# Inverting 16 by 16 blocks instead of 8 by 8 on VectorE, with other costs in the list scheduler

## The chip, the cores and the metric

The kernel runs on one core of one Trainium2 chip. The metric is device time in microseconds (us); a kernel is run several times and the median counts. A profile is one further execution, recorded by the hardware profiler.

The engines are TensorE (PE, with its weight loads as PEld), VectorE (DVE), ScalarE (ACT), GpSimd (POOL) and SyncE (SP), which here issues nearly all DMAs. In the kernel's code they are `T`, `V`, `S`, `G` and `Y`.

## What is computed

One decoder layer for 256 prompt tokens (one sequence) and 64 sample tokens (8 sequences of 8), 320 tokens in all. The model width is 2048. A single projection `h @ w_in` feeds two branches, whose outputs are projected, gated, added and projected once more. Branch A is a delta rule over 16 heads of 64:

```python
def step(s, inp):
    r_t, w_t, k_t, v_t, kk_t, a_t = inp
    sa = jnp.einsum('nhvk,nhk->nhv', s, kk_t)
    s = (s * w_t[:, :, None, :]
         - sa[..., None] * (kk_t * a_t)[:, :, None, :]
         + v_t[..., None] * k_t[:, :, None, :])
    return s, jnp.einsum('nhvk,nhk->nhv', s, r_t)
...
merged = (jax.nn.sigmoid(p[..., OFF_GA:OFF_GB]) * (y_a @ proj_a)
          + jax.nn.sigmoid(p[..., OFF_GB:]) * (y_b @ proj_b))
y = x + merged @ w_out
```

Branch B is a gated linear recurrence over 8 heads of 128. All inputs and outputs are fp32.

## The kernel before

**Weights.** Every large product is made of three: weights and activations are each split into a high and a low part of the type fp32r (`whi`, `wlo`, `hhi`, `hlo`), and high x high, high x low and low x high are added in PSUM. A block of weights is 1024 x 128: SyncE loads `raw` (512 KB), ScalarE rounds it to `whi`, VectorE subtracts to get `wlo`, and TensorE runs 24 matmuls of 128 x 128 by 320 tokens into `mps`. There are three buffers of each.

**Stages.** After a start (norm and transposes of x) comes the *recorded stage*, which goes to about 690 us. It runs over p = 0 to 7; one p is two heads of branch A and one of branch B and is called a head below. For each p eight column tiles of `w_in` (two blocks each) are streamed, then come `rwkv(p, ...)` and `hgrn(p, ...)`. Seven tiles of gate columns (`NFILL` + `NLATE`) follow as filler. Then the last stage streams the other gates, `proj_a`, `proj_b` and `w_out`; it needs `ya` and `yb`, the branches' outputs, of all heads.

**The order of the recorded stage.** All its instructions are first recorded by `Recorder`, with the regions that each reads and writes. `Recorder.order` then plays them through in time: each has a `cost` (how long its engine is taken) and a `lat` (how long until another may use its result), PE products that are not streamed have a `margin`, and for each engine the ready instruction with the highest `worth` (for most the `rank`, the length of the longest chain behind it) is taken next. Streamed matmuls keep their order and fill TensorE where nothing else is ready. The resulting order of each engine is fixed in the program, SyncE's DMAs included. All these instructions are issued at L1465, so the profile gives that line for the stage, and groups are told apart by tile names. Tags shared by several tiles show as the tag (`uB`, `uE`, `uK`, `pp`, `big`).

**The inverse.** Within a chunk of 64 tokens (and within a sample sequence of 8) the delta rule needs the inverse of I + N, N strictly triangular. The steps in `rwkv`:

- `g2` holds the masked products of keys, `nd` their part for the inverse, `M` its transpose.
- GpSimd masks the diagonal blocks of 8 (`lows`, a tile of `pp`), VectorE sums them into `dn` (128 partitions x 6 x 8). Two DMAs through a scratch tensor in DRAM turn that into `nb`: 96 partitions, one whole 8 by 8 block each.
- VectorE makes `y8` = `id8` - `nb`, and inverts: four instructions join 1 by 1 blocks to 2 by 2, then two products and two reduces join 4 by 4 blocks to 8 by 8 (`t64`, `p16`).
- Two DMAs bring the blocks back as `ye`; GpSimd spreads them into `yd` (prompt) and `ys` (samples), ScalarE copies `yd` into `yz`.
- A loop over `sz` in 8, 16, 32 joins blocks of `sz` to blocks of twice that on TensorE: two transposes of `yd`, a copy to `xt` (tag `uB`), the product `M` x `yz` (`pP`), the masked product `pp` on VectorE, the product `xt` x `pp` (`pD`), two subtractions from `yz` on VectorE and, except the last time, two copies to `yd` on ScalarE.

Then the chunks follow one another (`rhs`, `uv`, the states `st`), and the result is normalised and gated into `ya`.

Of the kernel before, what the change touches and what calls it, by code (L numbers as in the profile page):

```python
# [67 lines left out]


class Recorder:  # L70
    APART, MARGIN, WAIT, OVER = 10, 250, 6000, 130
    LAT = {"PE": 215, "V": 45, "S": 45, "G": 80, "Y": 0}

    def __init__(self, engines, is_big):
        self.real, self.ops, self.spans, self.is_big = engines, [], {}, is_big
# [10 lines left out]
    def add(self, eng, name, fn, args, kw):  # L86
        o = Op()
        o.eng, o.fn, o.args, o.kw, o.n = eng, fn, args, kw, len(self.ops)
        aps = [x for x in (*args, *kw.values()) if hasattr(x, "start_partition")]
        out = aps[0]  # L90
        free = 1
        for d in out.shape[1:]:
            free *= d
        o.uses = []
        for j, x in enumerate(aps):
            t_ = x.tensor
            if "DRam" in type(t_).__name__:
# [12 lines left out]

        two = sum("PSUM" not in str(x.space) for x in aps[1:] if tuple(x.shape[1:]) != (1,)) > 1
        o.hold = two and eng in "VG"
        o.port = two and eng == "V" or eng == "G" and "dma" not in name
        if eng == "PE":
            lhs, rhs = aps[1], aps[2]
            o.cols = 1
            for d in lhs.shape[1:]:
                o.cols *= d
            n = 1
            for d in rhs.shape[1:]:  # L120
                n *= d
# [12 lines left out]
        elif eng == "V":  # L134
            two = name in ("tensor_scalar", "tensor_copy") and all(not u[5] for u in o.uses)
            o.cost = (free / 2 if two else free) / 0.96 + (150 if two else 157)
            if two:
                o.hold = o.port = True
            if any(tuple(x.shape[1:]) == (1,) and free > 1 for x in aps[1:]):
                o.cost += 55  # L140
            if name == "tensor_tensor_scan":
                o.cost = 2 * free / 0.96 + 157
        elif eng == "S":
            o.cost = (150 if name == "copy" else 200) + free / 1.2
            if name == "copy" and not o.uses[1][5]:
                o.cost += 40
            if any(tuple(x.shape[1:]) == (1,) and free > 1 for x in aps[1:]):
                o.cost += 60
        elif eng == "G":
            o.cost = 950 if "dma" in name else 95 + free * 0.88 if name == "memset" else 200 + free * 1.66  # L150
            if "dma" in name:
                o.lat = 4500
        else:
            o.cost, o.lat = 380, 2600 if any(u[0].startswith("scr") for u in o.uses) else 5500
        self.ops.append(o)
        return o

    def link(self):
# [42 lines left out]
        for o in self.ops:  # L201
            o.npred = len(preds[o.n])
            for q, data in preds[o.n].values():
                q.succ.append((o, data))
        for o in reversed(self.ops):
            o.rank = o.cost + max((q.rank + (o.lat if data else 0) for q, data in o.succ), default=0)
        for members in groups.values():
# [4 lines left out]
    def order(self):  # L212
# [12 lines left out]
        at = {}  # L225
# [4 lines left out]
        def choose(e):  # L230
# [12 lines left out]
            if e == "PE":  # L243
# [13 lines left out]
                if o.stream:  # L257
                    o = min((o for o in pool if o.stream), key=lambda o: o.n)
                return max(t_, o.ready), o
            can = [o for o in q if (at_[o] if e in port else o.ready) <= t_ + 30]  # L260

            def worth(o):
                if o.block is None:
                    return (3 if e == "Y" else 1), o.rank
                slack = (at[o.block] - gone) * 147 + max(0, free["PE"] - t_)
                return (2 if slack < 4500 else 0), -o.n
            return t_, max(can, key=worth)

        while left:
            t_, o = min((choose(e) for e in ready if ready[e]), key=lambda x: (x[0], x[1].eng == "V"))  # L270
# [27 lines left out]
def hybrid_step(ctx, tc, x_prompt, x_sample, state_rwkv, state_hgrn, state_shift, norm_g, w_in,  # L298
# [80 lines left out]
    with tc.tile_pool(name="start", bufs=1) as st, \  # L379
# [60 lines left out]
            G.affine_select(out=ap, in_=ap, pattern=pattern, compare_op=ALU.is_ge, fill=fill,  # L440
                            base=base, channel_multiplier=cm)

        id8 = ctile([128, 64], "id8")
        G.memset(id8, 0.0)
        G.memset(id8[:, 0:64:9], 1.0)
        id32 = ctile([128, 32], "id32")
        G.tensor_add(id32, id64[:, 0:32], id64[:, 32:64])


        low_ = HS[0]  # L450
        lvs = st.tile([128, 3, 32], F32, name="lvs")
        lvz = ctile([128, 3, 2, 32], "lvz")
        seqm = ctile([128, NSEQ], "seqm")
        mk_lv = {}
        V.memset(lvs[low_], 1.0)
        G.memset(seqm[low_], 1.0)
        for n, sz in enumerate((8, 16, 32)):
            mk_lv[sz] = lvz[:, n]
            lv = lvs[low_, n].rearrange("p (b s) -> p b s", s=sz)
            nb = 32 // sz  # L460
# [6 lines left out]
        V.memset(lvz[low_, :, 1], 0.0)  # L467
        V.memset(lvz[HS[1], :, 0], 0.0)
        G.tensor_copy(seqm[HS[1]], seqm[low_])

# [314 lines left out]
    def rwkv(p, r, k, vp, za):  # L785
# [132 lines left out]
        for h in range(2):  # L918
            for c_ in range(2):
                S.copy(M[HS[c_], :, h], ps[HS[h], :256].rearrange("p (a c s) -> p a c s", c=2, s=64)[:, :, c_])  # L920


        lows = at("lows", (128, 4, 8, 8), tag="pp")
        each = lambda n: seqm[:, None, :, None].to_broadcast([128, n, 8, 8])
        G.tensor_mul(lows, nd.rearrange("p a h (b j) -> p (a h) b j", j=8), each(4))
        dn = at("dn", (128, 6, 8))
        V.tensor_reduce(dn[:, 0:4], lows.rearrange("p c b j -> p c j b"), axis=mybir.AxisListType.X, op=ALU.add)
        V.tensor_reduce(dn[0:64, 4:6], g2[0:64, 4, 0].rearrange("p h (b j) -> p h j b", j=8),
                        axis=mybir.AxisListType.X, op=ALU.add)
        there = lambda t_: t_.rearrange("(c p) j -> p c j", c=6)  # L930
        whole = lambda t_: t_.rearrange("(q i) j -> q (i j)", i=8)
        Y.dma_start(there(scratch[0]), dn)
        nb = at("nb", (96, 64), tag="pp")
        Y.dma_start(nb, whole(scratch[0]))
        y8 = at("y8", (96, 64))
        V.tensor_sub(y8, id8[:96], nb)

        t8 = nb
        four = lambda o_, *d: bass.AP(y8.tensor, y8.offset + o_, [y8.ap[0], *d])
        t4 = t8[:, 0:4].rearrange("p (a i) -> p a i", i=2)  # L940
        V.tensor_mul(t4, four(2, [36, 2], [8, 2]), four(19, [36, 2], [0, 2]))
        V.tensor_add(four(3, [36, 2], [8, 2]), four(3, [36, 2], [8, 2]), t4)
        V.tensor_mul(t4, four(10, [36, 2], [1, 2]), four(1, [36, 2], [0, 2]))
        V.tensor_add(four(2, [36, 2], [1, 2]), four(2, [36, 2], [1, 2]), t4)
        t64 = t8.rearrange("p (i j k) -> p i j k", j=4, k=4)
        p16 = at("p16", (96, 4, 4))
        V.tensor_mul(t64, four(4, [8, 4], [0, 4], [1, 4]), four(36, [0, 4], [1, 4], [8, 4]))
        V.tensor_reduce(p16, t64, axis=mybir.AxisListType.X, op=ALU.add)
        V.tensor_mul(t64, four(0, [8, 4], [0, 4], [1, 4]),
                     p16.rearrange("p k j -> p j k")[:, None].to_broadcast([96, 4, 4, 4]))  # L950
        V.tensor_reduce(four(4, [8, 4], [1, 4]), t64, axis=mybir.AxisListType.X, op=ALU.add)
        Y.dma_start(whole(scratch[1]), y8)
        ye = at("ye", (128, 6, 8))
        Y.dma_start(ye, there(scratch[1]))

        ys = at("ys", (128, 2, 64))
        wide = lambda t_: t_.rearrange("p h (b j) -> p h b j", j=8)
        spread = lambda x, n: ye[x, 4 * (n == 2):4 * (n == 2) + n, None, :].to_broadcast([x.stop - x.start, n, 8, 8])
        G.tensor_mul(yd.rearrange("p a h (b j) -> p (a h) b j", j=8), spread(slice(0, 128), 4), each(4))
# [14 lines left out]

        for sz in (8, 16, 32):
            xt = at("xt", (128, 4, 64), tag="uB")
            px = aps("pX")
            for cp in range(2):  # L980
# [703 lines left out]
```

## Time and profile before

| | |
|---|---|
| median of 3 runs | 1105.28 us (1103.35 to 1106.14) |
| profiled execution | 1104.54 us |
| its span, from the first to the last instruction | 1102.8 us |
| mean granted TensorE clock | 0.996 |
| TensorE busy | 1081.3 us, 98% of the span |
| VectorE busy | 750.6 us, 68% |
| ScalarE busy | 680.1 us, 62% |
| GpSimd busy | 154.6 us, 14% |

Durations of the trace are those of the profiled execution. A row that groups instructions has their line, engine, operation, tiles (out<-in), shape and count, then the busy time in us and the mean duration in ns, then the idle time of the engine just before them and what ended most of it. A row of the order of time begins with the start and the duration in us. A wait row has the total in us, the number of waits and the longest.

### The profile page before, as it was taken

How to read it: one execution, taken by the hardware profiler on the slowest of the kernel's cores; microseconds unless marked ns; L12 is line 12 of the kernel's file. 1: busy time of each engine (PE TensorE's matmuls, PEld its weight loads, DVE VectorE, ACT ScalarE, POOL GpSimd, SP SyncE). 2: the span in 40 equal slices, each digit the busy share in tenths (PEclk: the TensorE clock that was granted, in tenths of full speed). 3: DMA queues.
4: the chain of work that ended last, by engine and by line, in shares of the span. 5: the costliest groups of instructions: out<-in, count | busy, mean ns of one | idle time of the engine just before them, and what ended most of it. 6: DMA issues, size and time to landing. Idle time of an engine off the chain costs nothing.

```text
span 1102.8 us, 23134 instructions
## 1 busy us (share of the span) xinstructions
PE 1081.3 (98%) x9020; PEld 1043.5 (95%) x9020; DVE 750.6 (68%) x1639; ACT 680.1 (62%) x1530; POOL 154.6 (14%) x328
## 2 busy tenths in 40 slices
PE   7999999999999999999999999999999999999996
PEld 6999999999998999999999999999999999998886
DVE  8878787888787788788887976644444444437532
ACT  8767776766865867857857867544444444435412
POOL 6421222311211211211311210000000000000000
PEclk9999999999999999999999999999999999999999
DMA  6743644654553554555445454555555555586502
GB/s 200 205 127 100 180 129 123 161 145 114 162 136 101 156 144 117 153 138 140 117 138 144 123 144 130 149 152 160 152 146 146 149 154 153 153 282 223 200 21 96
DMA packets 298386, 161.62 MB, mean 147 GB/s; under 512 B 37341, under 2 KB 288480, under 8 KB 297700
## 3 DMA queue, kind: packets, MB, share of 16 engines
q1 hardware_dynamic: 297908, 158.83, 50.1%
q8 instruction: 71, 1.16, 0.4%
q10 hardware_dynamic: 368, 1.31, 0.3%
q14 instruction: 39, 0.32, 0.1%
HBM read 149.41 MB, written 10.70 MB: 145 GB/s over the span
## 4 chain that ended last, share of the span: by engine, by line
PE 95%; ACT 2%; DMA 1%; DVE 1%; issue 0%; POOL 0%; DVEq 0%; SPq 0%; ACTq 0%
PE mps L1465 45%; PE a L1465 9%; PE mps L362 5%; PE mps L364 5%; PE mps L363 5%; PE b L1465 3%; PE po L1555 3%; PE po L1556 3%; PE po L1557 3%; PE ppa L363 2%; PE ppa L364 2%; PE ppa L362 2%; PE ppb L362 2%; PE ppb L363 2%; PE ppb L364 2%; PE y L1465 1%
## 5 line engine op out<-in xcount | busy, mean ns | idle before, releaser
L1465 PE MATMUL mps<-hhi,wlo 128*128 128x320 f32 x1136 | 358.9, 316 | 0.0
L1465 PE MATMUL mps<-hhi,whi 128*128 128x320 f32 x1136 | 357.0, 314 | 0.5 <-ACT pad L1465 0.5
L1465 PE MATMUL mps<-hlo,whi 128*128 128x320 f32 x1136 | 357.3, 314 | 0.0
L1465 PEld LDWEIGHTS mps<-hhi,wlo 128*128 128x128 f32 x1136 | 213.7, 188 | 2.3 <-issue 1.5
L1465 PEld LDWEIGHTS mps<-hhi,whi 128*128 128x128 f32 x1136 | 213.8, 188 | 2.0 <-issue 0.8
L1465 PEld LDWEIGHTS mps<-hlo,whi 128*128 128x128 f32 x1136 | 213.7, 188 | 1.5 <-issue 0.8
L1465 DVE TENSOR_TENSOR wlo<-raw,whi 128x1024 fp32r<-128x1024 f32 x140 | 173.6, 1240 | 21.0 <-ACT whi L1465 19.7
L1465 ACT CAST whi<-raw 128x1024 fp32r<-128x1024 f32 x140 | 146.4, 1045 | 63.2 <-PE mps L1465 56.7
L352 ACT CAST whi<-raw 128x1024 fp32r<-128x1024 f32 x82 | 86.0, 1049 | 147.8 <-PE mps L363 94.3
L353 DVE TENSOR_TENSOR wlo<-raw,whi 128x1024 fp32r<-128x1024 f32 x82 | 100.5, 1225 | 110.1 <-ACT whi L352 110.1
L362 PE MATMUL mps<-hhi,whi 128*128 128x320 f32 x400 | 123.9, 310 | 1.0 <-ACT whi L352 1.0
L364 PE MATMUL mps<-hhi,wlo 128*128 128x320 f32 x400 | 123.7, 309 | 0.2 <-DVE wlo L353 0.2
L363 PE MATMUL mps<-hlo,whi 128*128 128x320 f32 x400 | 123.8, 309 | 0.0
L362 PEld LDWEIGHTS mps<-hhi,whi 128*128 128x128 f32 x400 | 75.1, 188 | 1.3 <-ACT whi L352 1.3
L364 PEld LDWEIGHTS mps<-hhi,wlo 128*128 128x128 f32 x400 | 75.1, 188 | 0.4 <-DVE wlo L353 0.4
L363 PEld LDWEIGHTS mps<-hlo,whi 128*128 128x128 f32 x400 | 75.2, 188 | 0.0
L1544 DVE TENSOR_TENSOR wlo<-raw,whi 128x1024 fp32r<-128x1024 f32 x32 | 38.4, 1222 | 36.0 <-ACT whi L1543 35.8
L1543 ACT CAST whi<-raw 128x1024 fp32r<-128x1024 f32 x32 | 33.1, 1052 | 47.7 <-PE po L1560 21.1
L1555 PE MATMUL po<-whi,mhi 128*128 128x512 f32 x128 | 50.0, 391 | 0.0
L1556 PE MATMUL po<-whi,mlo 128*128 128x512 f32 x128 | 50.0, 391 | 0.0
L1557 PE MATMUL po<-wlo,mhi 128*128 128x512 f32 x128 | 50.0, 391 | 0.0
L362 PE MATMUL ppa<-yah,whi 128*128 128x320 f32 x128 | 40.1, 314 | 0.1
(444 smaller groups left out, 2100.2 us busy)
## 6 DMA issues: line engine op xcount, KB each, us to landing
raw<-in_w_in_dram SPq DMA_DIRECT2D x194, 512.0 KB
raw<-in_w_out_dram SPq DMA_DIRECT2D x32, 512.0 KB
raw<-in_proj_a_dram SPq DMA_DIRECT2D x16, 512.0 KB
raw<-in_proj_b_dram SPq DMA_DIRECT2D x16, 512.0 KB
s<-in_state_hgrn_dram SPq DMA_DIRECT2D x8, 512.0 KB
out_dram<-s SPq DMA_DIRECT2D x8, 512.0 KB
s<-in_state_rwkv_dram SPq DMA_DIRECT2D x8, 256.0 KB
out_dram<-s SPq DMA_DIRECT2D x8, 256.0 KB
```

The source lines that it names most:

```text
L352: S.copy(hi[:, ks], raw[:, ks])
L353: sub.tensor_sub(lo[:, ks], raw[:, ks], hi[:, ks].bitcast(F32))
L362: T.matmul(dst, hi[:, q, :], xhi[:, k, :], start=(k == 0), stop=False)
L363: T.matmul(dst, hi[:, q, :], xlo[:, k, :], start=False, stop=False)
L364: T.matmul(dst, lo[:, q, :], xhi[:, k, :], start=False, stop=(k == nk - 1))
L1465: o.fn(*o.args, **o.kw)
L1543: S.copy(hi, raw)
L1544: V.tensor_sub(lo, raw, hi.bitcast(F32))
L1555: T.matmul(pt, h, hi, start=first, stop=False)
L1556: T.matmul(pt, l, hi, start=False, stop=False)
L1557: T.matmul(pt, h, lo, start=False, stop=end)
```

## The change

Two things are changed together.

The blocks that VectorE inverts are 16 by 16. `own16` replaces the mask of 8; the tiles become `dn` 128 x 6 x 16, `nb` and `y16` 48 x 256, `ye` 128 x 6 x 16, and the scratch tensors 768 x 16. A sample sequence's 8 by 8 blocks are inverted in pairs, as 16 by 16 blocks with zeros beside them. The negation of `nb` is a tensor_scalar, and GpSimd writes the ones of the diagonal. The 2 by 2 step covers twice the columns; the product-and-reduce step runs for n = 4 on two blocks and for n = 8 on one. The loop on TensorE runs over 16 and 32 only.

In `Recorder`, 85 ns (VectorE), 100 ns (ScalarE) and 65 ns (GpSimd) are taken off the cost of each instruction and added to its latency, which is also counted on every edge to another engine; the other latencies and the overlap of the port that VectorE and GpSimd share (`OVER`) get new values. A tensor_reduce costs as many elements as it reads. In the choice of the next instruction, one that becomes ready within 150 ns (`AHEAD`) may be preferred to one that is ready now; a shorter one goes first only where it ends at most 60 ns (`SLIP`) past the preferred one's start.

```diff
 class Recorder:
-    APART, MARGIN, WAIT, OVER = 10, 250, 6000, 130
-    LAT = {"PE": 215, "V": 45, "S": 45, "G": 80, "Y": 0}
+    APART, MARGIN, WAIT, OVER = 10, 250, 6000, 45
+    AHEAD, SLIP = 150, 60
+    LAT = {"PE": 215, "V": 40, "S": 40, "G": 65, "Y": 0}
+    DRAIN = {"V": 85, "S": 100, "G": 65}
...
+        if eng in self.DRAIN and not o.dma:
+            if name == "tensor_reduce":
+                n = 1
+                for d in aps[1].shape[1:]:
+                    n *= d
+                o.cost += (n - free) / 0.96
+            o.cost -= self.DRAIN[eng]
+            o.lat += self.DRAIN[eng]
...
-                q.succ.append((o, data))
+                q.succ.append((o, data or q.eng in self.DRAIN and q.eng != o.eng))
...
-            can = [o for o in q if (at_[o] if e in port else o.ready) <= t_ + 30]
+            if e not in port:
+                at_ = {o: max(now, o.ready) for o in q}
...
-            return t_, max(can, key=worth)
+            best = max((o for o in q if at_[o] <= t_ + self.AHEAD), key=worth)
+            if at_[best] > t_ + 30:
+                short = [o for o in q if at_[o] <= t_ + 30 and at_[o] + o.cost <= at_[best] + self.SLIP]
+                if short:
+                    best = max(short, key=worth)
+            return t_, best
...
-        id8 = ctile([128, 64], "id8")
-        G.memset(id8, 0.0)
-        G.memset(id8[:, 0:64:9], 1.0)
...
-        for n, sz in enumerate((8, 16, 32)):
+        for n, sz in enumerate((16, 32)):
...
+        own16 = ctile([128, 4], "own16")
+        G.tensor_add(own16, seqm[:, 0:8:2], seqm[:, 1:8:2])
...
-        lows = at("lows", (128, 4, 8, 8), tag="pp")
+        lows = at("lows", (128, 4, 4, 16), tag="pp")
...
-        dn = at("dn", (128, 6, 8))
+        dn = at("dn", (128, 6, 16))
...
-        nb = at("nb", (96, 64), tag="pp")
+        nb = at("nb", (48, 256), tag="pp")
         Y.dma_start(nb, whole(scratch[0]))
-        y8 = at("y8", (96, 64))
-        V.tensor_sub(y8, id8[:96], nb)
+        y16 = at("y16", (48, 256), tag="uK")
+        V.tensor_scalar(y16, nb, -1.0, 0.0, op0=ALU.mult, op1=ALU.add)
+        G.memset(y16[:, 0:256:17], 1.0)
...
-        t64 = t8.rearrange("p (i j k) -> p i j k", j=4, k=4)
-        p16 = at("p16", (96, 4, 4))
-        V.tensor_mul(t64, four(4, [8, 4], [0, 4], [1, 4]), four(36, [0, 4], [1, 4], [8, 4]))
-        V.tensor_reduce(p16, t64, axis=mybir.AxisListType.X, op=ALU.add)
-        V.tensor_mul(t64, four(0, [8, 4], [0, 4], [1, 4]),
-                     p16.rearrange("p k j -> p j k")[:, None].to_broadcast([96, 4, 4, 4]))
-        V.tensor_reduce(four(4, [8, 4], [1, 4]), t64, axis=mybir.AxisListType.X, op=ALU.add)
-        Y.dma_start(whole(scratch[1]), y8)
-        ye = at("ye", (128, 6, 8))
+        for n in (4, 8):
+            t_ = at("t3", (48, n, n, n), tag="big")
+            pw_ = at("p64", (48, n, n), tag="uQ")
+            for o_ in range(0, 16, 2 * n):
+                at_ = lambda i, j: 17 * o_ + 16 * i + j
+                V.tensor_mul(t_, four(at_(0, n), [16, n], [0, n], [1, n]), four(at_(n, n), [0, n], [1, n], [16, n]))
+                V.tensor_reduce(pw_, t_, axis=mybir.AxisListType.X, op=ALU.add)
+                V.tensor_mul(t_, four(at_(0, 0), [16, n], [0, n], [1, n]),
+                             pw_.rearrange("p k j -> p j k")[:, None].to_broadcast([48, n, n, n]))
+                V.tensor_reduce(four(at_(0, n), [16, n], [1, n]), t_, axis=mybir.AxisListType.X, op=ALU.add)
+        Y.dma_start(whole(scratch[1]), y16)
+        ye = at("ye", (128, 6, 16))
...
-        for sz in (8, 16, 32):
+        for sz in (16, 32):
...
-    scratch = [scr.tile([768, 8], F32, name=f"scr{j}", tag=f"scr{j}") for j in range(2)]
+    scratch = [scr.tile([768, 16], F32, name=f"scr{j}", tag=f"scr{j}") for j in range(2)]
```

More of the change, by code (lines that the diff above doesn't have):

```diff
@@ L450, in hybrid_step @@
         low_ = HS[0]
-        lvs = st.tile([128, 3, 32], F32, name="lvs")
-        lvz = ctile([128, 3, 2, 32], "lvz")
+        lvs = st.tile([128, 2, 32], F32, name="lvs")
+        lvz = ctile([128, 2, 2, 32], "lvz")
         seqm = ctile([128, NSEQ], "seqm")
@@ L920, in rwkv @@
                 S.copy(M[HS[c_], :, h], ps[HS[h], :256].rearrange("p (a c s) -> p a c s", c=2, s=64)[:, :, c_])
-        lows = at("lows", (128, 4, 8, 8), tag="pp")
-        each = lambda n: seqm[:, None, :, None].to_broadcast([128, n, 8, 8])
-        G.tensor_mul(lows, nd.rearrange("p a h (b j) -> p (a h) b j", j=8), each(4))
-        dn = at("dn", (128, 6, 8))
+        lows = at("lows", (128, 4, 4, 16), tag="pp")
+        each = lambda n: own16[:, None, :, None].to_broadcast([128, n, 4, 16])
@@ L927, in rwkv @@
+        G.tensor_mul(lows, nd.rearrange("p a h (b j) -> p (a h) b j", j=16), each(4))
+        dn = at("dn", (128, 6, 16))
         V.tensor_reduce(dn[:, 0:4], lows.rearrange("p c b j -> p c j b"), axis=mybir.AxisListType.X, op=ALU.add)
-        V.tensor_reduce(dn[0:64, 4:6], g2[0:64, 4, 0].rearrange("p h (b j) -> p h j b", j=8),
+        V.tensor_reduce(dn[0:64, 4:6], g2[0:64, 4, 0].rearrange("p h (b j) -> p h j b", j=16),
                         axis=mybir.AxisListType.X, op=ALU.add)
         there = lambda t_: t_.rearrange("(c p) j -> p c j", c=6)
-        whole = lambda t_: t_.rearrange("(q i) j -> q (i j)", i=8)
+        whole = lambda t_: t_.rearrange("(q i) j -> q (i j)", i=16)
@@ L932, in rwkv @@
         Y.dma_start(there(scratch[0]), dn)
-        nb = at("nb", (96, 64), tag="pp")
+        nb = at("nb", (48, 256), tag="pp")
         Y.dma_start(nb, whole(scratch[0]))
-        y8 = at("y8", (96, 64))
-        V.tensor_sub(y8, id8[:96], nb)
+        y16 = at("y16", (48, 256), tag="uK")
+        V.tensor_scalar(y16, nb, -1.0, 0.0, op0=ALU.mult, op1=ALU.add)
+        G.memset(y16[:, 0:256:17], 1.0)
         t8 = nb
-        four = lambda o_, *d: bass.AP(y8.tensor, y8.offset + o_, [y8.ap[0], *d])
@@ L940, in rwkv @@
[L940 to L944, printed above, removed]
-        t64 = t8.rearrange("p (i j k) -> p i j k", j=4, k=4)
-        p16 = at("p16", (96, 4, 4))
-        V.tensor_mul(t64, four(4, [8, 4], [0, 4], [1, 4]), four(36, [0, 4], [1, 4], [8, 4]))
@@ L948, in rwkv @@
-        V.tensor_reduce(p16, t64, axis=mybir.AxisListType.X, op=ALU.add)
-        V.tensor_mul(t64, four(0, [8, 4], [0, 4], [1, 4]),
-                     p16.rearrange("p k j -> p j k")[:, None].to_broadcast([96, 4, 4, 4]))
-        V.tensor_reduce(four(4, [8, 4], [1, 4]), t64, axis=mybir.AxisListType.X, op=ALU.add)
-        Y.dma_start(whole(scratch[1]), y8)
-        ye = at("ye", (128, 6, 8))
+        four = lambda o_, *d: bass.AP(y16.tensor, y16.offset + o_, [y16.ap[0], *d])
+        t4 = t8[:, 0:8].rearrange("p (a i) -> p a i", i=2)
@@ new lines, in rwkv @@
+        V.tensor_mul(t4, four(2, [68, 4], [16, 2]), four(35, [68, 4], [0, 2]))
+        V.tensor_add(four(3, [68, 4], [16, 2]), four(3, [68, 4], [16, 2]), t4)
+        V.tensor_mul(t4, four(18, [68, 4], [1, 2]), four(1, [68, 4], [0, 2]))
+        V.tensor_add(four(2, [68, 4], [1, 2]), four(2, [68, 4], [1, 2]), t4)
+        for n in (4, 8):
[8 more added lines that the diff above has]
+                V.tensor_reduce(four(at_(0, n), [16, n], [1, n]), t_, axis=mybir.AxisListType.X, op=ALU.add)
@@ L954, in rwkv @@
+        Y.dma_start(whole(scratch[1]), y16)
+        ye = at("ye", (128, 6, 16))
         Y.dma_start(ye, there(scratch[1]))
         ys = at("ys", (128, 2, 64))
-        wide = lambda t_: t_.rearrange("p h (b j) -> p h b j", j=8)
-        spread = lambda x, n: ye[x, 4 * (n == 2):4 * (n == 2) + n, None, :].to_broadcast([x.stop - x.start, n, 8, 8])
-        G.tensor_mul(yd.rearrange("p a h (b j) -> p (a h) b j", j=8), spread(slice(0, 128), 4), each(4))
+        wide = lambda t_: t_.rearrange("p h (b j) -> p h b j", j=16)
@@ L960, in rwkv @@
+        spread = lambda x, n: ye[x, 4 * (n == 2):4 * (n == 2) + n, None, :].to_broadcast([x.stop - x.start, n, 4, 16])
+        G.tensor_mul(yd.rearrange("p a h (b j) -> p (a h) b j", j=16), spread(slice(0, 128), 4), each(4))
         G.tensor_mul(wide(ys[0:64]), spread(slice(0, 64), 2), each(2)[0:64])
```

## The prediction

> **What bounds the kernel now.** I read the page first, then busy time by stretch, then what TensorE waits for, then the order of time around one level of the inverse.
>
> ```profile
> span 1102.8 us, 23134 instructions
> ...
> PE 1081.3 (98%) x9020; PEld 1043.5 (95%) x9020; DVE 750.6 (68%) x1639; ACT 680.1 (62%) x1530; POOL 154.6 (14%) x328
> ```
>
> TensorE is busy for 98% of the span. Ends of matmuls are modelled, so this alone proves little; the stretches say more. The first row below is one head of the recorded stage, the second the last head with its fill, the third the stretch just behind the stage.
>
> ```profile
> core 0: us, PE busy (x) PEld busy (x) DVE busy (x) ACT busy (x) POOL busy (x), PEclk, DMA share, GB/s
> 467.00:544.00 77.00, 75.97 (x759) 73.97 (x759) 62.03 (x163) 56.34 (x147) 16.12 (x33) 1.00 0.50 137
> 621.00:692.00 71.00, 70.37 (x712) 68.19 (x710) 51.74 (x130) 51.88 (x132) 6.73 (x8) 1.00 0.49 135
> ...
> 695.16:698.57 3.41, 3.41 (x15) 3.41 (x14) 2.62 (x5) 2.96 (x6) 0.00 (x0) 0.50 0.56 159
> ```
>
> In a head of 77 us TensorE is idle for 1.0 us, while VectorE has 15.0 us to spare (77.0 - 62.0) and ScalarE 20.7. So a head lasts as long as its matmuls, and work on the other engines costs nothing until a wait of TensorE grows. Those waits between 30 and 690 us, without one of 0.4, and the longest just behind the stage:
>
> ```profile
> PE b L1465 <- issue: 1.9, 1, 1.9
> PE a L1465 <- DVE yz L1465: 1.2, 2, 0.6
> PE a L1465 <- POOL yd L1465: 1.0, 1, 1.0
> PE a L1465 <- ACT uv L1465: 0.5, 1, 0.5
> PE mps L1465 <- ACT pad L1465: 0.5, 1, 0.5
> ```
>
> ```profile
> PE mps L362 <- ACT whi L352: 1.0, 1, 1.0
> ```
>
> They come to 5.1 us in the stage. The 1.9 has no releaser in the profile and no plan made it; the other 3.2 are places where TensorE, whose order is fixed beforehand, came to an operand later than planned (yz and yd are the inverse's own). The 1.0 us behind the stage stands where TensorE has used up its filler and the last head's ya is not there. The half granted clock follows it (0.50 in the third row): 15 matmuls in 3.41 us, where a step of 0.147 us (below) would give 23, so 8 x 0.147 = 1.2 us. This end costs 2.2 us together.
>
> **The change, part by part. A level of the inverse goes.** The pass with sz = 8 has, per head, two transposes, four instructions for pP and four for pD (fp32 products, two passes each). Head 1, in order of time on TensorE:
>
> ```profile
> 167.48 0.31 PE L1465 MATMUL mps<-hhi,whi 128*128 128x320 f32 x1
> 167.63 0.38 PE L1465 MATMUL a<-ident,yd 128*128 128x128 f32 x2
> 167.76 0.39 PE L1465 MATMUL mps<-hlo,whi 128*128 128x320 f32 x1
> 167.99 0.31 PE L1465 MATMUL mps<-hhi,wlo 128*128 128x320 f32 x1
> ...
> 169.32 0.30 PE L1465 MATMUL mps<-hhi,wlo 128*128 128x320 f32 x1
> ...
> 169.76 0.31 PE L1465 MATMUL mps<-hhi,wlo 128*128 128x320 f32 x1
> 169.90 0.61 PE L1465 MATMUL a<-pp,uB 128*128 128x128 f32 x4
> 170.26 0.39 PE L1465 MATMUL mps<-hhi,whi 128*128 128x320 f32 x1
> 170.50 0.30 PE L1465 MATMUL mps<-hlo,whi 128*128 128x320 f32 x1
> ...
> 173.28 0.38 PE L1465 MATMUL a<-ident,yd 128*128 128x128 f32 x2
> ```
>
> ```profile
> L1465 PE MATMUL a<-pp,uB 128*128 128x128 f32 x96 | 16.2, 279 | 0.4 <-issue 0.4
> L1465 PE MATMUL a<-ident,yd 128*128 128x128 f32 x48 | 9.3, 274 | 1.0 <-POOL yd L1465 1.0
> ```
>
> Durations overlap, so I go by starts. Three streamed steps from 169.32 to 169.76 are 0.44: 0.147 each. From 167.48 to 167.99 there are two streamed matmuls (0.294) and the transposes: 0.51 - 0.29 = 0.22. From 169.76 to 170.50 there are two and the four of pD: 0.74 - 0.29 = 0.45, with the slower step right behind the burst. pP has the same four instructions of the same shape, another 0.45. A level takes 1.11 us of TensorE, and the counts (96 = 8 heads x 3 levels x 4, 48 = 8 x 3 x 2) say that 8 such levels go: **8.9 us, all of it on the engine that sets the end.**
>
> **VectorE and ScalarE.** Rows for what goes and comes:
>
> ```profile
> L1465 DVE TENSOR_TENSOR yz<-yz,a 64x128 f32<-64x128 f32 x48 | 13.6, 284 | 5.9 <-PE a L1465 5.1
> L1465 DVE TENSOR_TENSOR s<-s,b 128x512 f32<-128x512 f32 x16 | 10.9, 682 | 0.2
> L1465 DVE TENSOR_TENSOR pp<-a,lvz 128x256 f32<-128x256 f32 x24 | 10.2, 425 | 10.4 <-PE a L1465 9.7
> L1465 DVE TENSOR_REDUCE dn<-pp 128x32 f32<-128x256 f32 x8 | 5.3, 659 | 4.0 <-POOL pp L1465 4.0
> L1465 DVE TENSOR_SCALAR f<-f,lbt 128x320 f32<-128x320 f32 x8 | 3.0, 377 | 0.3 <-ACT f L1465 0.3
> ```
>
> ```profile
> L1465 DVE TENSOR_TENSOR y<-id,pp x8: 214/216/223, 72.2 to 633.2; 96x64 f32<-96x64 f32 x8
> L1465 DVE TENSOR_REDUCE p<-pp x8: 207/208/216, 73.5 to 637.4; 96x16 f32<-96x64 f32 x8
> L1465 DVE TENSOR_TENSOR pp<-y,p x8: 260/264/270, 75.3 to 637.8; 96x64 f32<-96x64 f32 x8
> ```
>
> ```profile
> L1465 ACT COPY yd<-yz 64x128 f32<-64x128 f32 x32 | 9.4, 295 | 9.0 <-DVE yz L1465 8.5
> L1465 ACT COPY uB<-a 128x256 f32<-128x256 f32 x24 | 9.0, 373 | 11.7 <-PE a L1465 11.6
> ```
>
> Gone per head: pp 0.43 and two yz 0.57 on VectorE; uB 0.37 and two yd 0.59 on ScalarE. The four 2 by 2 instructions and the two reduces to dn keep their number of inputs. The subtraction from id8 (0.22) becomes a tensor_scalar of 256 (below 0.377: about 0.34), +0.12. The 4 by 4 step (product, reduce, twice: 0.264 + 0.208 + 0.264 + 0.208 = 0.94) is done twice: +0.94. The 8 by 8 step is new and has 512 elements, of which no row exists. Its products lie between the plain one of 512 (0.682) and the rate of the strided dn reduce (0.659 for 256, so up to 1.3). The nearest row is the strided product of 64: 0.264 against 0.216 plain, 0.75 ns more an element, so 0.68 + 512 x 0.00075 = 1.07; I take that. Its reduces: 0.208 for 64 and some 1.04 ns for each of 448 more, 0.67, at most 1.3. Together 2 x 1.07 + 2 x 0.67 = 3.48 (2.7 to 5.2). VectorE: 3.48 + 0.94 + 0.12 - 1.00 = **+3.5 us a head** (2.8 to 5.3), 62.0 to about 65.5 in 76: hidden by the spare 15.0. What is late if that cover goes is the wlo of a block, which the stream needs every 24 x 0.147 = 3.5 us.
>
> **The chain.** The level takes 173.28 - 167.63 = 5.65 us of latency. In come 3.48 + 0.94 + 0.12 and the diagonal that GpSimd now writes between two VectorE steps (no row has it; two crossings and a memset, 0.2 to 1 us, I take 0.4): 4.9, up to 7.3. So a head's chain is 0.7 us shorter, or up to 1.7 longer. In heads 0 to 6 the next head's blocks cover either. In the last, ya already comes late: TensorE gets 1.1 us quicker and ya 0.7, so up to 0.4 is lost there, up to 2.8 with the dear price.
>
> **The queues.** The four scratch transfers a head keep their number and double their bytes, 24 to 48 KB; runs of 8 floats become runs of 16 and the 96 rows 48.
>
> ```profile
> 239.35 2.98 DMA scr<-y
> ...
> 242.36 4.79 DMA ye<-scr
> ```
>
> ```profile
> SPq L1465 <- DVE wlo L1465: 203.1, 69, 9.3
> ```
>
> At 137 GB/s of the head 24 KB more are 0.18 us each, 0.7 a head at most in the chain. I take 0, as the transfers are mostly fixed latency, and nothing waits but the chain. SP issues in order: weight loads stand behind a scratch store that waits for VectorE. It waits for buffers anyway, 203 us in 69 waits, so a store that is late by less than such a wait moves no load. Removed constants (id8, a mask) and the added own16 lie in the start on GpSimd; nothing in the waits above follows them: 0.
>
> **The scheduler.** It moves nothing by itself; the order of the whole stage comes out anew. Its new costs take 85 ns off each VectorE instruction and 100 off each on ScalarE and give them back as latency. The trace bears this out:
>
> ```profile
> 233.14 0.22 DVE L1465 TENSOR_TENSOR y<-id,pp 96x64 f32<-96x64 f32 x1
> 233.28 0.28 DVE L1465 TENSOR_TENSOR F<-F 128x128 f32<-128x128 f32 x1
> ```
>
> The second starts 0.08 us before the first has ended. [...] The wait for a chain's next step (150 ns ahead) can leave VectorE idle for up to 0.15 us a step; with some 10 us to spare a head, 0 to TensorE. What better costs are worth is bounded by the waits: 3.2 + 2.2 = 5.4 at best (7.3 with the unexplained 1.9), and below by as much in new ones. I take a third, 1.9: two of five waits stand on yz, of which a third of the steps go, but new orders bring new misses.
>
> Sum: the profiled execution took 1104.5 us (span 1102.8 and 1.7 around it), 0.8 under the median of 1105.3. 1104.5 - 8.9 - 1.9 = 1093.7, or 1094.5 from the median: **1094 us**.
>
> **The rivals.**
> Nearly all waits go: 1104.5 - 8.9 - 7.3 = 1088. For it: waits on yz and uv are of the kind that truer costs mend. Against: the 1.9 has no releaser.
> The last chain decides: ya comes 3 us later (1.7 from the dear products, the rest behind other VectorE work), and TensorE waits for that and the 1.1 it saved: 1104.5 - 8.9 + 4.1 = 1099.7. For it: the 1.0 us wait and the half clock already stand there.
> The new order is worse: the waits double, 5.1 + 2.2: 1104.5 - 8.9 + 7.3 = 1102.9, no change that counts. Against: costs nearer to the trace.
> The change doesn't do what it says: VectorE, not TensorE, paces the heads and the level comes back as waits, 1104. Against: 1.0 us idle against 15.0.
> Slower: VectorE cannot overlap as planned. 163 instructions x 0.085 = 13.9 us a head would be promised and not there; spare is 76 - 65.5 = 10.5, so TensorE waits 3.4 a head for wlo: 1104.5 - 8.9 + 27 = 1123. It decides from (8.9 + 3.3) / 8 = 1.5 us of wait a head. Against: the overlap above, which this trace has whether it is planned or not.
>
> **How the numbers follow.** About 0.3%, 3.3 us, can be told from no change, so faster is under 1102.0. Forecast 0.60 (1091 to 1097); nearly all waits go 0.10; last chain 0.12; worse order 0.10; VectorE paces 0.03; slower rival 0.05. Faster 0.82, same 0.13, slower 0.05. Leaving out the last three (0.18), the range is 1087 to 1101.
>
> **What would show it.** Right: yd transposes x32 for x48, pp,uB x64 for x96, yz x32; a head of about 76 us; VectorE 65 to 66 of it; products of 48x512 near 1.07 us. Wrong: waits of TensorE on wlo or whi within the stage, over 7 us of waits in all, or a longer gap before ya at the stage's end.

## The result and the profile after

The changed kernel takes 1134.0 us (median of 4 runs, 1132.3 to 1134.9), the kernel before 1105.1 in the same job: a ratio of 1.026, 95% interval 1.024 to 1.028. It is 29 us slower, where 11 us faster was forecast. First the head of its page, to be held against the 1102.8 us, 1081.3, 750.6 and 680.1 of before.

```profile
span 1132.8 us, 23031 instructions
PE 1092.5 (96%) x8940; PEld 1034.0 (91%) x8940; DVE 779.1 (69%) x1679; ACT 685.1 (60%) x1506; POOL 170.6 (15%) x333
```

TensorE has 80 matmuls fewer (8940 for 9020) and is still busy for 11 us more. Busy time by stretch: one head of the stage, the last head with its fill, and the stretch just behind the stage.

```profile
482.00:562.00 80.00, 76.43 (x742) 71.89 (x742) 69.31 (x173) 57.49 (x145) 20.20 (x35) 1.00 0.48 132
642.00:724.00 82.00, 80.74 (x756) 76.30 (x755) 46.44 (x102) 51.92 (x122) 5.37 (x5) 1.00 0.49 139
725.20:728.61 3.41, 2.96 (x21) 2.92 (x21) 3.28 (x5) 3.41 (x7) 0.00 (x0) 1.00 0.61 191
```

A head lasts 80 us instead of the 76 that were forecast, and TensorE (first pair of numbers behind the length) is idle for 3.6 us of it instead of 1.0. (The stretches are cut by hand. From one copy `za<-mps` to the next, over seven heads, a head takes 80.3 us on the mean, before 73.5.) VectorE (third pair) is far from full: 69.3 of 80. The clock (1.00) plays no part. The first `ppa` matmul, which ends the stage, starts at 724.8 us instead of 693.8; behind it both kernels need 408 to 409 us. So the 30 us of the span lie in the recorded stage. Next, what TensorE waits for there (waits of 1.8 us and more in total):

```profile
PE a L1484 <- POOL yd L1484: 6.3, 6, 1.7
PE a L1484 <- DVE v L1484: 3.6, 4, 1.0
PE a L1484 <- DVE uv L1484: 2.6, 7, 0.9
PE b L1484 <- DVE k L1484: 2.5, 6, 0.5
PE a L1484 <- DVE yz L1484: 2.3, 6, 0.5
PE b L1484 <- ACT i L1484: 1.8, 3, 0.9
```

With the smaller ones they come to 25.3 us (before: 6.7, the same way counted), many small waits on operands of the two branches, none on `whi` or `wlo`. Waits of over 7 us in all were one of the prediction's signs of being wrong. That is 18.6 us more; the rest stands nowhere in this view, since the modelled end of a streamed matmul (313 ns for a step of 147) hides a stall of up to 166 ns behind it. How such a wait comes about is seen in VectorE's order of time ahead of the second wait on `v`, and in TensorE's:

```profile
291.51 0.76 DVE L1484 TENSOR_TENSOR fq<-f,fh 32x8 fp32r<-32x8 f32 x2
292.29 0.34 DVE L1484 CAST fq<-f 32x8 fp32r<-32x8 f32 x2
292.65 1.23 DVE L1484 TENSOR_TENSOR wlo<-raw,whi 128x1024 fp32r<-128x1024 f32 x1
293.80 0.49 DVE L1484 TENSOR_TENSOR uK<-uK,uQ 128x320 f32<-128x320 f32 x1
294.20 0.49 DVE L1484 TENSOR_TENSOR dif<-pad 128x328 f32<-128x328 f32 x1
294.61 0.49 DVE L1484 TENSOR_TENSOR uQ<-uK,uA 128x320 f32<-128x320 f32 x1
295.01 0.48 DVE L1484 SCALAR_TENSOR_TENSOR v<-dif,cols,pad 128x256 f32<-128x256 f32 x1
```

```profile
294.28 0.31 PE L1484 MATMUL mps<-hhi,wlo 128*128 128x320 f32 x1
295.55 0.44 PE L1484 MATMUL a<-ident,v 128*128 128x128 f32 x2 [0.96 <-DVE v L1484]
```

VectorE is never idle here; it is late. Behind `wlo` each instruction starts 80 to 90 ns before the one ahead of it has ended, as the new plan counts on. The two pairs of `fq`, each instruction on 32 partitions and in another group of 32 than the last, overlap nothing: 292.29 is 20 ns after the end of the first pair (291.51 + 0.76), 292.65 is 20 ns after the end of the second. The plan's own start of each, as `Recorder.order` computes it when the kernel is built, taken off the start in the trace, shows it step by step:

```
start in the trace   tile    later than planned by
291.51               fq      48.60 us
291.68               fq      48.69
292.29               fq      48.74
292.46               fq      48.84
292.65               wlo     48.97
293.80 to 295.90     uK, dif, uQ, v, uA, v, uA   48.96 to 48.97
```

(The stage starts 25 us into the span, so the plan is 24 us behind by now.) Four starts in other partitions than those of the instruction ahead cost 0.37 us that the plan did not have (48.97 - 48.60); the seven that follow in the same partitions cost nothing. Over all back-to-back pairs of the kernel before, sorted by whether the first input and the output start in the same 32 partitions as those of the instruction ahead (gap: start minus end of the one ahead, median over the stage, pairs where the second does not read what the first wrote):

```
engine    same start partitions     other start partitions
VectorE   -82 ns (648 pairs)        +31 ns (295 pairs)
ScalarE   -97 ns (568)              +24 ns (298)
GpSimd    -50 ns  (40)              +41 ns  (69)
```

Lastly the changed steps themselves:

```profile
L1484 PE MATMUL a<-pp,uB 128*128 128x128 f32 x64 | 11.7, 286 | 0.0
L1484 PE MATMUL a<-ident,yd 128*128 128x128 f32 x32 | 6.7, 290 | 6.5 <-POOL yd L1484 6.3
L1484 DVE TENSOR_TENSOR big<-uK,uQ 48x512 f32<-48x512 f32 x8 | 9.2, 1146 | 0.1
L1484 DVE TENSOR_TENSOR big<-uK 48x512 f32<-48x512 f32 x8 | 8.5, 1058 | 0.2
L1484 DVE TENSOR_REDUCE uK<-big 48x64 f32<-48x512 f32 x8 | 5.4, 678 | 0.3
L1484 DVE TENSOR_REDUCE uQ<-big 48x64 f32<-48x512 f32 x8 | 5.4, 677 | 0.2
L1484 DVE TENSOR_TENSOR yz<-yz,a 64x128 f32<-64x128 f32 x32 | 9.1, 283 | 0.6
```

The level is gone and VectorE's new steps cost what was forecast for them.

### The profile page after: what moved, and what is told of

Read it like the earlier page. It is cut to its first block, busy times and chain, and to the rows that moved or that the text cites. A ratio compares the mean times of both kernels' runs of the same rounds, so it can differ in the third digit from the quotient of the medians.

```text
span 1132.8 us, 23031 instructions
## 1 busy us (share of the span) xinstructions
PE 1092.5 (96%) x8940; PEld 1034.0 (91%) x8940; DVE 779.1 (69%) x1679; ACT 685.1 (60%) x1506; POOL 170.6 (15%) x333
## 3 DMA queue, kind: packets, MB, share of 16 engines
q8 instruction: 70, 1.15, 0.4%
## 4 chain that ended last, share of the span: by engine, by line
PE 56%; DVE 24%; ACT 11%; DMA 5%; issue 3%; POOL 0%; SPq 0%; DVEq 0%; ACTq 0%
PE mps L1484 14%; DVE wlo L1484 7%; PE mps L378 5%; PE mps L379 5%; PE mps L380 5%; PE a L1484 4%; PE po L1574 3%; PE po L1575 3%; PE po L1576 3%; DVE big L1484 2%; PE ppa L379 2%; PE ppb L378 2%; PE ppb L379 2%; PE ppb L380 2%; PE ppa L380 2%
## 5 line engine op out<-in xcount | busy, mean ns | idle before, releaser
L1484 POOL TENSOR_TENSOR big<-bk,seq 128x512 f32<-128x512 f32 x8 | 31.6, 3953 | 61.9 <-DVE uK L1484 46.4
```

The source lines that it names most:

```text
L1484: o.fn(*o.args, **o.kw)
```

## The experiments

Theories, by the letters of the expectations. **D**: the drains (the ns in `DRAIN`), taken off the costs, are promised to the plan and not there on the chip. **B**: the blocks load VectorE too much. **A**: the wait for a chain's next step wastes the engines' time. **H**, formed after the first round: an instruction does start before the end of the one ahead (by 82 ns on VectorE in the table above), except where its start partitions differ (31 ns after it). **R**: costs other than the drains are wrong too. Medians below stand beside 1104.9 to 1106.5 us of the kernel before in the same jobs. Where a small difference between two jobs counts, the ratios to the kernel before are compared. As the order is fixed beforehand, a run's stage is the plan's own length plus what the chip falls behind it; both are given for every run in a table at the end.

**The two halves: the blocks with the scheduler of before, and the scheduler of after with blocks of 8.**

```diff
# e1_blocks: class Recorder as before
-    AHEAD, SLIP = 150, 60
-    DRAIN = {"V": 85, "S": 100, "G": 65}
...
# e2_sched: class Recorder as after, rwkv() as before
-        for n, sz in enumerate((16, 32)):
+        for n, sz in enumerate((8, 16, 32)):
```

> The 16 by 16 blocks with the scheduler of before. Theory D (the drains: the new costs take 85 to 100 ns off every VectorE and ScalarE instruction, about half of them do not overlap, so the plan promises results too early and TensorE waits in its fixed order): the blocks alone bring the level's 8.9 us, 1093 to 1100 us. Theory B (the blocks: VectorE's longer inverse, its strided products and GpSimd's diagonal make the operands late): 1125 to 1136 us, with TensorE waiting on yd. Theory A (the wait for a chain's next step): as D, 1093 to 1100.

> The new scheduler with the 8 by 8 blocks. Theory D and theory A: 1125 to 1135 us, the whole loss, with the waits of TensorE on v, uv, k and yz as in the changed kernel. Theory B: 1098 to 1106 us.

e1_blocks took 1125.0 us (ratio 1.018, 1.016 to 1.020), e2_sched 1135.4 (1.027, 1.026 to 1.029). Both halves lose by themselves, and together no more than the worse one. The scheduler does as D says (and A; 0.4 us above their range). The blocks alone were not expected by D or A to lose. Their time lies at the edge of B's range, but B's sign, waits on `yd`, is missing: those come to 0.3 us. (D's "about half" is too much: of the pairs in the table above, about a third do not overlap.) TensorE's waits in the stage with e1_blocks, and a stretch of its busy time:

```profile
PE mps L1468 <- ACT pad L1468: 17.0, 4, 5.8
PE mps L1468 <- ACT za L1468: 5.4, 4, 1.4
```

```profile
420.00:560.00 140.00, 128.40 (x1311) 125.07 (x1312) 110.39 (x275) 95.12 (x249) 23.36 (x51) 0.94 0.44 120
```

Here a few long holes stand where a new head's streamed tiles wait for `pad` to be read out, and the granted clock is 0.94 in this stretch. VectorE has 29.6 us to spare in these 140. But the plan thinks otherwise: without overlap it counts 584 us of VectorE (570 before) in a stage of 674 (655 before), and its own TensorE idles 40.4 us (12.7 before), with single holes of 5.7, 6.4 and 5.9 us in the heads p = 5, 6 and 7. The holes are planned, and the order carries them to the chip.

**The wait for a chain's next step, taken out of the changed kernel.**

```diff
-    AHEAD, SLIP = 150, 60
+    AHEAD, SLIP = 30, 60
```

> The changed kernel with AHEAD = 30, which is the old rule of choice, and the new costs. Theory A: 1093 to 1103 us. Theory D and theory B: 1128 to 1137 us.

1149.1 us (1.040, 1.038 to 1.041): 15 us worse without it, and above D's range too. A is wrong: the waiting helps.

**The drains left in the cost.**

```diff
-    LAT = {"PE": 215, "V": 40, "S": 40, "G": 65, "Y": 0}
-    DRAIN = {"V": 85, "S": 100, "G": 65}
+    LAT = {"PE": 215, "V": 45, "S": 45, "G": 80, "Y": 0}
+    DRAIN = {"V": 0, "S": 0, "G": 0}
```

> The changed kernel with the drains at 0 and the latencies of before (45, 45, 80), so that each instruction occupies its engine for its whole duration; the wait for a chain's next step, the dearer reduces and the port's 45 ns stay. Theory D: 1093 to 1104 us, with under 10 us of visible TensorE waits in the stage. Theory A: 1125 to 1135. Theory B: 1125 to 1135.

1108.2 us (1.003, 1.002 to 1.004): 26 of the 29 us come back. The drains are the cause of the loss; but the time is 4 us above D's range, with 12.7 us of TensorE's waits, and the forecast is not reached. The plan again counts no overlap, as in e1_blocks, and has 20.3 us of TensorE idle in it.

**The drains given back only where the chip takes them.** `held_` compares the group of 32 partitions in which the first input and the output start, for SBUF and PSUM apart, with the last one of the same engine. The lines that use it in the choice of the next instruction are not shown.

```diff
+            for u in o.uses:
+                o.quads.setdefault((u[4], u[5]), u[1] // 32)
...
+        def held_(o):
+            if any(last[o.eng].get(k, v) != v for k, v in o.quads.items()):
+                return self.DRAIN[o.eng] + self.HELD      # HELD = 20
+            return 0
...
-            start = max(t_, o.ready)
+            start = max(t_, o.ready, free[o.eng] + held_(o))
+            last[o.eng].update(o.quads)
```

> The changed kernel (16 by 16 blocks, drains taken off the costs, wait for the next step), but the plan gives the drain back, with 20 ns more, to each instruction whose input or output starts in another group of 32 partitions than the one before it on its engine. Theory H (the drains do overlap, but not behind such a change of partitions, and that alone is what the plan of the changed kernel had wrong): 1084 to 1097 us, faster than before, with TensorE's visible waits in the stage under 8 us. Rival R (the promise is broken elsewhere too, by strided products, GpSimd's copies and the shared port): 1104 to 1125.

1098.5 us (0.994, 0.992 to 0.995), 36 us faster than the changed kernel from this rule alone, and faster than before; it just misses the range. TensorE's waits in the stage are 5.8 us in place of 25.3, and mostly these:

```profile
PE a L1495 <- POOL yd L1495: 4.0, 5, 2.2
```

Is it this rule, or would any smaller promise have done? A smaller drain for all instructions alike was not run, but the plan's own starts, taken off the trace's, tell where the delay arises. In the changed kernel VectorE falls behind its plan by 55.9 us over the stage. Of these, 30.3 come at its 332 starts in other partitions that follow within 60 ns of the instruction ahead (91 ns each); the 874 such starts in the same partitions win 6.3 back; the rest comes where VectorE sits idle. On ScalarE it is 34.5 of 54.9 us, at 354 starts. In e5_held the same sums are -1.7 us on VectorE and -0.7 on ScalarE.

**The same scheduler with blocks of 8** (`rwkv` as before):

> The same plan with the 8 by 8 blocks. Theory H: 1094 to 1104 us, some 9 us above the 16 by 16 blocks, the level's price on TensorE. Rival R: above 1110. If the larger blocks cost VectorE more than they save TensorE, this run is the faster of the two.

1101.0 us (0.996, 0.994 to 0.997). With this plan the larger blocks gain 2.5 us, not the 9 that H expected.

**No drains and no wait ahead; and no drains with blocks of 8.**

```diff
# e7_now: as e4_drain, with
-    AHEAD, SLIP = 150, 60
+    AHEAD, SLIP = 30, 60
# e8_drain8: as e4_drain, with rwkv() as before
```

> 16 by 16 blocks, no drains, and AHEAD = 30, the old rule of choice. If the wait for a chain's next step makes the 17 us between the blocks with the old scheduler (1125) and the blocks without drains (1108): 1120 to 1132. If the dearer reduces and the port's 45 ns make it: 1105 to 1112.

> 8 by 8 blocks, no drains, with the wait for a chain's next step. If the larger blocks lose because a plan without overlap thinks VectorE full (its costs for the stage go from 573 to 595 us, in a stage of some 650): 1094 to 1103, faster than the 1108 of the 16 by 16 blocks. If the blocks bring the level's 8.9 us under any plan: 1114 to 1119.

e7_now took 1130.1 us (1.022, 1.021 to 1.024), e8_drain8 1097.0 (0.992, 0.991 to 0.994). So the wait ahead is worth 22 us with the large blocks (1130.1 to 1108.2) and, with the small ones, at most 8 (1105.1 to 1097.0, where the dearer reduces, `OVER`'s new value and the edges to other engines change too). Under costs without overlap, blocks of 8 beat blocks of 16 by 11 us. And with blocks of 8 the plan that knows of the partitions (e6_held8, 1101.0) is 4 us slower than the one that counts no overlap at all: both plans are 646.8 us long, and the chip falls further behind the first. So the rule, with the overlap that it leaves, is worth 10 us with the large blocks (e4_drain to e5_held) and nothing with the small ones; why is open.

**Two more costs put right** on top of e5_held: VectorE's inputs with a stride (the products of 48x512: 1.06 and 1.15 us in the changed kernel), and GpSimd's products of 256 (`yd`, `lows`: 1.00 and 1.01 us there).

```diff
+        if eng == "V" and any(len(x.ap) > 1 and abs(x.ap[-1][0]) >= 4 and x.ap[-1][1] > 1 for x in aps[1:]):
...
+            o.cost += 0.75 * max(n, free)
+        if eng == "G" and name == "tensor_mul" and free == 256:
+            o.cost += 350
```

> The plan that knows of the partitions, 16 by 16 blocks, and with costs nearer to the trace for what was still late in it: 0.75 ns more an element for VectorE instructions whose input strides by 16 bytes or more (the products of the 8 by 8 step are planned at 690 ns and take 1060 to 1150), 350 ns more for GpSimd's products of 256. If those late steps cost the 16 by 16 blocks the rest of the level's price (TensorE waits 4.1 us for yd in the run without them): 1091 to 1096. If it isn't the plan any more but VectorE's real load: 1097 to 1100, no change.

> The same costs with the 8 by 8 blocks. If only the blocks' new steps were mis-sized: 1099 to 1103, as without the costs, so that the larger blocks are worth 6 us or more with a true plan. If GpSimd's products mattered for both: 1095 to 1098.

e9_costs, with blocks of 16, took 1095.0 us (0.991, 0.989 to 0.992), e10_costs8, with blocks of 8, 1098.3 (0.994, 0.992 to 0.995), between its two expectations. R is right in part: these costs were wrong too, and were worth 3.5 and 2.7 us. e9_costs beats both kernels; over the best run with blocks of 8, e8_drain8, it gains 2 us. The head of its page, and TensorE's waits of 0.8 us and more in the stage:

```profile
span 1092.6 us, 22994 instructions
...
PE 1070.0 (98%) x8940; PEld 1033.1 (95%) x8940; DVE 775.9 (71%) x1679; ACT 681.1 (62%) x1506; POOL 154.4 (14%) x333
```

```profile
PE a L1502 <- issue: 3.0, 2, 2.3
PE b L1502 <- issue: 1.6, 1, 1.6
PE b L1502 <- ACT uv L1502: 1.2, 1, 1.2
PE a L1502 <- POOL yd L1502: 0.8, 2, 0.5
```

The same 8940 matmuls as in the changed kernel keep TensorE busy for 22.5 us less. Waits of this size on VectorE are gone, those on `yd` are down from 4.0 to 0.8, and 4.6 us have no releaser.

**The drains of one engine alone** taken off the cost.

```diff
# e11_v
+    DRAIN = {"V": 85, "S": 0, "G": 0}
# e12_s
+    DRAIN = {"V": 0, "S": 100, "G": 0}
```

> The changed kernel with the drains taken off VectorE alone (85 ns; ScalarE and GpSimd at 0, with their old latencies). Without any drains it took 1108, with all 1134. If VectorE's promise is the one that is missed: 1125 to 1135. If both engines share it: 1108 to 1124. Taken off one engine, the drains could also help where none are counted: below 1106 would say that ScalarE's alone did the harm.

> The changed kernel with the drains taken off ScalarE alone (100 ns; VectorE and GpSimd at 0). If ScalarE's promise is the one that is missed: 1125 to 1135. If both engines share it: 1108 to 1124. If VectorE's alone did the harm: about 1108, as with no drains at all.

VectorE's alone: 1110.0 us (1.003, 1.002 to 1.004); ScalarE's alone: 1122.8 (1.013, 1.011 to 1.016). By the ratios, against e4_drain with none (1.0026), VectorE's cost 0.1 us, ScalarE's 12 and all of them 26. This is no clean division: giving VectorE its drains also takes the planned holes away (next table), so its harm may in part be paid for by that; its lag is twice that of e4_drain. That ScalarE's promise is broken as well is shown; the shares of the two stay open.

**Plan and lag.** Plan: the length of the stage that `Recorder.order` computes; idle: its own TensorE idle time; lag: by how much the chip's VectorE has fallen further behind the plan between the first and the last sample of its recorded order (every 60th instruction). All in us.

```
run         blocks  median   plan   idle   lag   plan + lag
before       8      1105.1   654.6  12.7  10.0   664.6
e1_blocks   16      1125.0   673.8  40.4  17.7   691.5
after       16      1134.0   638.3   6.1  55.8   694.1
e2_sched     8      1135.4   646.8   6.1  46.5   693.3
e3_ahead    16      1149.1   638.3   6.1  69.6   707.9
e4_drain    16      1108.2   653.9  20.3  15.6   669.5
e7_now      16      1130.1   683.0  49.7  13.3   696.3
e8_drain8    8      1097.0   646.8   6.1   8.6   655.4
e5_held     16      1098.5   638.3   6.1  18.4   656.7
e6_held8     8      1101.0   646.8   6.1  13.2   660.0
e9_costs    16      1095.0   638.3   6.1  15.4   653.7
e10_costs8   8      1098.3   646.8   6.1  10.5   657.3
e11_v       16      1110.0   638.3   6.1  30.9   669.2
e12_s       16      1122.8   649.4  16.0  35.9   685.3
```

The sum must follow the median (real time is planned time and delay): the median less the sum is 438.7 to 442.1 us in eleven of the runs. In e1_blocks, e7_now and e12_s it is 433.5 to 437.5, and there the time behind the stage is 2 to 5 us shorter. What the sum tells is where a run loses. e1_blocks and e7_now lose in the plan, after, e2_sched and e3_ahead on the chip, e12_s some in both. By its own plan the changed kernel is the best of all, 16.3 us shorter than before; the chip falls 45.8 us further behind it than it did.

## Why the prediction was wrong

**The step that failed: "The scheduler. ... The trace bears this out."** One pair of VectorE instructions that overlap was taken for all of them. The row was right and 648 pairs of the same trace are of its kind; 295 others, those that change start partitions, are not (nine in ten of them start 13 ns or more after the end of the one ahead). For ScalarE's 100 ns the prediction had no row at all, and these alone cost 12 us in e12_s. The trace of before had them in plain sight, in rows such as these of VectorE's order of time:

```profile
639.81 0.28 DVE L1465 TENSOR_TENSOR ks<-ks,q 128x128 f32<-128x128 f32 x1
640.01 0.22 DVE L1465 TENSOR_TENSOR qz<-es,q 128x64 f32<-128x64 f32 x1
640.15 0.22 DVE L1465 TENSOR_TENSOR es<-es,f 128x64 f32<-128x64 f32 x1
...
650.11 0.60 DVE L1465 TENSOR_TENSOR yz<-yz,a 64x128 f32<-64x128 f32 x2 [0.91 <-PE a L1465]
650.74 0.29 DVE L1465 TENSOR_TENSOR F<-F 128x128 f32<-128x128 f32 x1
```

`qz` and `es` start 80 ns before the end of the one ahead. The two halves of `yz`, which start at partition 0 and 64, take 0.60 us together, twice a single one (284 ns) and some more, and `F` starts 30 ns after them. e5_held shows that this is the cause: with the rule in the plan, and nothing else changed, 36 us go. The prediction weighed its row against a slower rival in which nothing overlaps, as if the two could not both be right. Sorted by start partitions, VectorE's pairs of the kernel before show both: a median of -82 ns where they are kept, of +31 ns where they change.

**The bounds of the scheduler's worth.** "What better costs are worth is bounded by the waits: 3.2 + 2.2 = 5.4 at best (7.3 with the unexplained 1.9), and below by as much in new ones" took the worst case from the size of today's waits. The bound that counts is how much the plan is promised: 85 to 100 ns for each instruction that is held. The prediction had that product, 13.9 us a head, in its slower rival.

**The slower rival** named the right kind of cause, VectorE that cannot overlap as planned, and left ScalarE out. Its place was wrong (no wait on `wlo`, but many short ones on `yd`, `v`, `uv`, `k`), and so was its threshold: it let the spare time of VectorE, 10.5 us a head, absorb the broken promise first. Spare time does not help an engine whose order is fixed by a plan that believes it has more: in the rows above VectorE works without a pause, but on other instructions than the one that TensorE waits for. It was priced at 1123 us and given too small a chance, because the one overlapping row stood against it.

**"VectorE: +3.5 us a head, hidden by the spare 15.0."** The size was right: 28.5 us more busy time in all (779.1 - 750.6; 28 were forecast), products of 1.06 and 1.15 us for 1.07, reduces of 0.68 for 0.67. The cover is there on the chip, but not in the plan of before, which counts no overlap at all; e1_blocks, whose plan lacks the cover, loses 20 us. How much of it that lack explains is not settled: the wait ahead takes 22 us away with the cover still missing (e7_now to e4_drain). Neither the old nor the new scheduler suits these blocks.

**"8.9 us, all of it on the engine that sets the end."** Counts x64 and x32 are as forecast. Its worth is best read where the plan is kept: e9_costs against e10_costs8, 3.3 us. In their profiled runs the stage from 30 us on is 654.6 and 658.9 us; less TensorE's waits (7.3 and 2.4, all gaps over 20 ns) it is 647.3 and 656.5, that is 9.2 us. So the matmuls did leave TensorE, about as sized; in these two executions 4.9 us come back as waits, 3.3 of it without a releaser (4.6 against 1.3). What these are stays open.

**The chain and the stage's end.** The half clock behind the stage is gone (1.00 at 725.20), and TensorE waits for `ya` twice, 0.4 us each. The 0.4 us for GpSimd's diagonal had no row behind it; the memset took 0.12 us, beside a VectorE step (it starts at 71.67 us in the first head, the step at 71.64), and held nothing up. But `yd`, which the prediction did not price, did: its product rose from 748 to 1004 ns and TensorE's waits for it have the largest sum, 6.3 us. **The queues**: right, no wait of TensorE in the stage ends on a transfer.

The forecast of 1094 us is about what the change gives, 1095.0, once the plan's costs are true (e9_costs). Near as it is, it is no proof of the sum: that kernel has other terms, the wait ahead above all, which the prediction put at 0 and which was worth 15 and 22 us where it alone was changed (e3_ahead, e7_now).

## What to carry to other kernels

Where a list scheduler's order is fixed in the program, a cost that is too low can do more harm than one that is too high, as it did here with both sizes of blocks (1134.0 for 1108.2, 1135.4 for 1097.0): the chip falls behind the plan, each engine then does the wrong thing first, and neither a low busy share nor a short plan shows it. A truer plan is no promise of a shorter time (e6_held8). Before a cost is lowered across a class of instructions, sort all pairs of the trace by what could divide them, start partitions here, and count; one row proves that a thing exists, not that it is the rule. Compare the plan's own start of each instruction with the trace: a lag that grows points at the wrong cost within a few rows.

## What was not expected of the hardware

ScalarE and GpSimd overlap and hold by start partitions as VectorE does (in the kernel before, medians of -97 against +24 ns and of -50 against +41 ns). And GpSimd's `big` product of 128x512 took 3953 ns on the mean after the change, 1196 before:

```profile
L1465 POOL TENSOR_TENSOR big<-bk,seq 128x512 f32<-128x512 f32 x8 | 9.6, 1196 | 14.7 <-ACT bk L1465 14.2 <-PE a L1465 0.4
L1484 POOL TENSOR_TENSOR big<-bk,seq 128x512 f32<-128x512 f32 x8 | 31.6, 3953 | 61.9 <-DVE uK L1484 46.4 <-ACT whi L1484 15.5
```

In time, GpSimd's row of after with what VectorE did from its start on:

```profile
159.99 3.96 POOL L1484 TENSOR_TENSOR big<-bk,seq 128x512 f32<-128x512 f32 x1 [7.73 <-DVE uK L1484]
```

```profile
159.74 1.21 DVE L1484 TENSOR_TENSOR wlo<-raw,whi 128x1024 fp32r<-128x1024 f32 x1
160.87 0.37 DVE L1484 TENSOR_SCALAR f<-f,lbt 128x320 f32<-128x320 f32 x1
161.17 1.21 DVE L1484 TENSOR_TENSOR wlo<-raw,whi 128x1024 fp32r<-128x1024 f32 x1
162.30 0.81 DVE L1484 TENSOR_TENSOR_SCAN F<-rs_b,w 128x320 f32<-128x320 f32 x1
163.15 1.15 DVE L1484 TENSOR_TENSOR w<-F 128x320 f32<-128x320 f32 x1
```

And in the kernel before, GpSimd's and VectorE's:

```profile
309.41 1.04 POOL L1465 TENSOR_TENSOR big<-bk,seq 128x512 f32<-128x512 f32 x1 [0.43 <-PE a L1465]
```

```profile
309.01 0.66 DVE L1465 TENSOR_REDUCE dn<-pp 128x32 f32<-128x256 f32 x1 [0.82 <-POOL pp L1465]
309.59 1.94 DVE L1465 TENSOR_TENSOR wlo<-raw,whi 128x1024 fp32r<-128x1024 f32 x1
```

In the rows of after a `wlo` is under way first: it keeps its 1.21 us, GpSimd's product lasts 3.96 us, until behind the scan, and `w`, next on VectorE, then takes 1.15 us (0.49 at 229.55 us in the kernel before). In those of before the product comes first: it takes 1.04 us and the `wlo` 1.94. No run here tried by itself what lengthens them. No wait of TensorE ends on this product.
